# Eleven RMS norms in a two-block model: rows scaled and then transposed, instead of products with a diagonal of 1/rms

## The chip, the cores and the metric

The kernel runs on one core of a Trainium2 chip. The metric is the device time of one execution in microseconds. Before the change three executions took 2910.46, 2912.77 and 2920.75 us; their median, 2912.77 us, is the time to beat. A difference of 0.5% is 14.6 us.

The engines are named as in the profile. PE is TensorE's matrix multiply and PEld its weight load, DVE is VectorE, ACT is ScalarE, POOL is GpSimd, and SP issues most loads.

## The reference, cut to what matters

The model has two blocks of two layers each, on 256 tokens of width 1024, all in float32. Each layer has a mixer and a feed-forward part, and each of these starts with the same step:

```python
def rms_norm(x, g):
    y = x * lax.rsqrt(jnp.mean(x * x, axis=-1, keepdims=True) + EPS)
    return y * g
h = rms_norm(x, norm_g) * (1.0 + scale) + shift      # scale, shift: per channel
proj = h @ w                                         # or the two products of SwiGLU, or the router
```

The sum of squares runs over the channels of one token, so 1/rms is one number per token. The gain, scale and shift are one number per channel. The matrix product that follows sums over channels, so `h` is wanted with channels on the 128 partitions, while `x` is kept with tokens on the partitions.

First block: layer 0 has a dense SwiGLU, layer 1 a mixture of eight experts. The second block has an attention-like mixer with a decaying state; it runs once over a second input (the context) and then over the first block's output (the latent stream).

## The kernel before, in words

`x` lies in four tiles `xs[t][n]`, token half `t` (128 tokens) by channel half `n` (512 channels); in the trace all of them are `xpt`. A norm has these steps, and there are eleven of them in the program:

- `rstd_rows` (L285): for each `t`, two squares with a running sum on ACT (L269, 128x512), then a Newton iteration on DVE for 1/rms (L275 to L281), one number per partition, `r[t]`.
- `scaled_t` (L334): DVE makes two diagonal 128x128 matrices, identity times `r[t]` (L338, tile `g0t` or `g1t`). For each of four groups `kp` of 256 channels PE makes four products, channel block by token half, of a block of `xs` with the diagonal (L344). That turns the block and scales it in one step, into one PSUM bank, 128 channels x 2 x 256 tokens.
- `affine_f32` (L311): A * ps + B per channel; DVE takes the first block of the group (L317) and ACT the second (L320). Both write one tile, and in the trace ACT follows DVE.
- `split` (L295): the result is divided in a rounded high part (ACT, L296) and a remainder (DVE, L297). Every large product is then three products (L234, L239, L240). The weights go through the same two lines as they arrive.

The order of work on every engine is set by a scheduler when the kernel is built: it takes the streams of instructions with their priorities and simulates time to decide what is issued next. The first block and the latent stream have the priority `lead`; the context stream and the vectors of modulation (L388, L410) are `fill`, put where the lead stream would wait. A change in one step can therefore move work in other places.

Tiles come from pools with fixed numbers of buffers. `scaled_t` takes its diagonal from the pool `g` (3 buffers). The tiles of `affine_f32` and `sumsq` come from the stream's pool `st`, and the high and low parts from `s`. In the first block and in the feed-forward part of the latent stream's first layer both are the pool `s0` with 12 buffers; the PSUM tiles come from pools of two banks or one.

Three other places matter below. L1512 to L1545 are the decaying attention of the context (PE L1512, exponentials on ACT at L1515, products L1535 and L1543, then L1575 and its square on ACT, L1577). L660 and L661 are the last step of the first block's mixer, with SiLU on ACT. L824 is the branch behind the router of the experts; behind it the first expert gathers its tokens (L909, L917) and loads its weights (L211).

Of the kernel before, what the change touches and what calls it, by code (L numbers as in the profile page):

```python
# [13 lines left out]
AF = mybir.ActivationFunctionType  # L14
# [48 lines left out]
class Res:  # L63
    """buffers of one stream: pools to take each kind of tile from (the listed ones in turn)"""
# [14 lines left out]
class Task:  # L79
    """a generator of instructions with its buffers and its place in the order of issue"""  # L80
# [15 lines left out]
class Builder:  # L96
# [36 lines left out]
    def use(self, res, key):  # L133
        """what is issued next belongs to the stream key, which takes its buffers from res"""
        if self.key is not None:
            self.prio[self.key] = self.tc.cur_priority
        self.R, self.key = res, key
        self.tc.cur_priority = self.prio[key]

# [77 lines left out]
    def wparts(self, dram):  # L217
        """loads dram [128, kt, n]; yields (first k, its k count, high part, low part), 4 KiB a part"""
        kt, n = dram.shape[1], dram.shape[2]
        st = max(1, 1024 // n)  # L220
        for k0 in range(0, kt, st):
            ks = min(st, kt - k0)
            src = self.wload(dram[:, k0:k0 + ks])
            h, l = (self.shaped(self.htile(), (ks, n)) for _ in range(2))
            self.split(h, l, src)
            yield k0, ks, h, l

    def mm3(self, ps, lh, ll, rh, rl, first, last, start=None):
        """ps += (lh + ll)^T (rh + rl) but for ll^T rl. start: whether the first product clears the marks of its bank;
        a second group in a bank starts without, after the first one's start"""  # L230
        mm = self.nc.tensor.matmul
        before = self.mark
        skip = start is not None
        i = mm(ps, lh, rh, start=start if skip else first, stop=False, skip_group_check=skip)  # L234
        if first:
            self.mark = i
            if start is False:
                self.tc.add_manual_dep(i.ins, before.ins.name, LATE, reason="order of the starts in a bank")
        mm(ps, lh, rl, start=False, stop=False, skip_group_check=skip)  # L239
        mm(ps, ll, rh, start=False, stop=last, skip_group_check=skip)  # L240

    def late(self, dma):
        """holds a load back until the product issued last has begun"""
        self.tc.add_manual_dep(dma.ins, self.mark.ins.name, LATE, reason="buffers of loads that could go far ahead")

# [1 line left out]
    def half_rsqrt(self, h, w):  # L247
        """1 / sqrt(2 h): three Newton steps, each of which turns the sign, from a negative guess"""
        V = self.nc.vector
        j = self.m1(w, I32)  # L250
        V.tensor_scalar(j, h.bitcast(I32), -0.5, float(0x5F3759DF - 0x400000 - 2 ** 31), op0=ALU.mult, op1=ALU.add)
        y = j.bitcast(F32)
        for _ in range(3):
            t, z = self.m1(w), self.m1(w)
            V.tensor_tensor(t, y, y, op=ALU.mult)
            V.tensor_tensor(t, t, h, op=ALU.mult)
            V.scalar_tensor_tensor(z, t, 1.5, y, op0=ALU.subtract, op1=ALU.mult)
            y = z
        return y
# [6 lines left out]
    def sumsq(self, x, out):  # L266
        """half the mean square of 512 of the 1024 columns"""
        j = self.st(512)
        self.nc.scalar.activation(j, x, AF.Square, scale=math.sqrt(0.5 / D), accum_out=out)  # L269

    def rstd(self, ss):
        """1/rms of tokens from the two halves of sumsq, [128, 2]: half_rsqrt with a number for each partition"""
# [12 lines left out]
    def rstd_rows(self, xs):  # L285
        """xs[t][n] [128,512] token-major; 1/rms per token, [128, 1] for each t"""
# [24 lines left out]
    def affine_f32(self, ps, kp, Aff, Bff, pool=None):  # L311
        """ps [128, 2, w] -> A*ps+B"""
# [21 lines left out]
    def scaled_t(self, xs, r):  # L334
        """channel-major xs * r, two blocks of channels at a time: products with diagonals of r"""
        dg = self.shaped(self.g1(), (2, 128))
        for t in range(2):
            self.nc.vector.tensor_scalar(dg[:, t], self.cc("ident"), r[t], None, op0=ALU.mult)  # L338
        for kp in range(4):
            ps = self.tp(2, 256)  # L340
            for q in range(2):
                k = 2 * kp + q
                for t in range(2):
                    self.nc.tensor.matmul(ps[:, q, t * 128:(t + 1) * 128],  # L344
                                          xs[t][k // 4][:, (k % 4) * 128:(k % 4 + 1) * 128], dg[:, t],
                                          start=True, stop=True)
            yield ps
# [6 lines left out]
    def conds(self):  # L354
        """silu of the three conditions, [128, 8, 32]: second block's two, first block's, zeros"""
# [16 lines left out]
    def gemv_step(self, m, c, A, name, l, grow):  # L372
        """a twelfth of the 6144 columns, in four column groups of the tensor engine"""
# [6 lines left out]
    def shift_scale(self, m, b, q, w_dram):  # L380
        """128 columns of each half of shift and scale: a column group each, then to channels on partitions"""
# [17 lines left out]
    def gate_row(self, m, b, half, w_dram, b_dram, grow):  # L399
        """half a gate, to a row in DRAM; each column group takes two of the eight k blocks.  # L400
        grow: function giving a DRAM row to multiply it by, or None"""
# [25 lines left out]
    def affine(self, m, which, i, gname):  # L427
        """(A, B) of g * (1 + scale), shift; which 0: mixer, 1: ffn"""
# [13 lines left out]
    def proj_parts(self, H, w, n, evac, kind="a"):  # L442
        """token-major [2 x 128, n] = H^T-stationary product with w [128, 8, n], in parts"""
# [19 lines left out]
    def ffn(self, H, gu, dn, nu, part, size=2):  # L463
        """SwiGLU over 256 tokens; part(section, t, n, psum) gets the product of each section of the hidden units"""
# [5 lines left out]
        def unit(u):  # L470
            """hidden units on partitions: gate and up blocks of 128, two of each to a bank"""
# [40 lines left out]
    def wout(self, M, w, korder, done, both=False):  # L512
        """mixed^T (M, 8 k blocks) @ w; done(n, [ps0, ps1]). both: the first k blocks for both halves of the columns
        before the others"""
# [29 lines left out]
    def mixer1(self, l, H, M):  # L544
# [10 lines left out]
        # convolution branch, channels on partitions  # L555
# [30 lines left out]
        # gating branch  # L586
# [26 lines left out]
        # gating products  # L613
# [25 lines left out]
        # convolution, layer norm over channels, swish  # L639
# [29 lines left out]
    def conv(self, l, glu):  # L669
        """depthwise convolution of the rows of glu. A product takes 32 channels at eight-apart taps on the rows of  # L670
        the tensor engine, by diagonals of the filters, to a column group of it"""
# [159 lines left out]
    def overflow(self, xn, Aff, Bff, pos, cw, G, xs):  # L831
        """slots 128..255 of each expert, in the buffers of the weights alone"""
# [49 lines left out]
    def scatter(self, pn, ws, G, y, yh, yl, DT, xs, n):  # L882
        """x += the rows of an expert, weighted and gated, back at their tokens"""
# [9 lines left out]
    def experts(self, xn, Aff, Bff, pos, cw, G, xs):  # L893
        """SwiGLU of each expert over the tokens whose slot lies in 0..127; x += their weighted and gated sum"""
# [4 lines left out]
        def gather(e):  # L899
            """tokens of an expert: one-hot rows the other way, their weights, the split inputs"""  # L900
# [134 lines left out]
    def plan(self, xs, m, m2, sh, task, G0, G1, G2, G3):  # L1035
        R0, R1, RM, RL = self.R0, self.R1, self.RM, self.RL

        def weave(t, *others, label="end"):
            """runs t to its label, with steps of the others between its own"""
# [3 lines left out]
        # second stream: modulation, then the whole first layer of the context  # L1043
# [15 lines left out]
        # first block  # L1059
# [30 lines left out]
    def first_end(self, xs):  # L1090
        """final norm of the first block"""
# [37 lines left out]
    def add_norm_gated(self, xs, yg, ss):  # L1129
        """x += rms_norm(y) * gate, from y * gate and the squares of y"""  # L1130
# [54 lines left out]
    def transpose4(self, src, n, w=128):  # L1185
        """src [128 tok, n * w] -> psum [w, n, 128]"""
# [5 lines left out]
    def lower_bounds(self):  # L1192
        """lower bounds of the forget gates of layer 1, one row per direction"""
# [19 lines left out]
    def mixer2(self, l, H, sh, M, kind):  # L1213
# [19 lines left out]
        def rot(o, ps, t):  # L1233
            """rotary embedding of 256 columns"""
# [88 lines left out]
        def take_logs():  # L1323
            """of the forget gates; with a lower bound of zero: log sigmoid(z) = min(z, 0) + log(1 - sigmoid(-|z|))"""
# [10 lines left out]
        def keys():  # L1335
            """keys with features on partitions: 4 (head, map) of 32 per group; the context's go to DRAM"""
# [111 lines left out]
    def state(self, d, lf, kt, v, sh):  # L1448
        """final state of one direction, [128 key, 4 heads, 128 value], to DRAM"""
# [142 lines left out]
    def mixed(self, M, k0, ps, now):  # L1592
        """two k blocks of the mixed branches, split now or by wout"""
# [8 lines left out]
    def transposed(self, ys, p0):  # L1602
        """columns p0 * 128.. of token-major ys[t] -> psum [128, 2, 256]"""
# [94 lines left out]
def _kchunks(w, n):  # L1698
    """[1024, C*n] -> [C, 128, 8, n]"""
# [4 lines left out]
def _level_patterns():  # L1704
    """[128, 2 directions, 9 * 128]: column t of a pattern sums the log decays between t and its block's middle.
    levels 64..8, outer for tokens 0..127, levels 4..1, outer for tokens 128..255"""
# [171 lines left out]
```

## Time and profile before

| | |
|---|---|
| three executions | 2910.46, 2912.77, 2920.75 us |
| span of the profiled execution, first to last instruction | 2917.1 us |
| mean granted clock of TensorE | 0.977 |
| PE busy | 2771.0 us, 95% |
| DVE busy | 2025.3 us, 69% |
| ACT busy | 1700.4 us, 58% |
| DMA, mean over the span | 244 GB/s |

The profile shows the execution from its first instruction to its last; it gives no time outside that span, and the span lies inside the range of the three timed executions, 0.15% above their median. A granted clock of 1.00 is the higher level, 2.4 GHz, and 0.5 the lower, 1.2 GHz. A float32 product of 128x128 is two records in the trace; a transpose is one.

### The profile page before, as it was taken

To read this page: it belongs to the slowest core of one execution; us is meant where nothing else is said; L and a number is where in the kernel's file an instruction comes from. 1 tells how busy PE (TensorE), PEld (TensorE's weight loads), DVE (VectorE), ACT (ScalarE), POOL (GpSimd) and SP (SyncE) were. 2 spreads that over 40 slices of the span, in tenths; PEclk is the share of its full clock that TensorE was granted. 3 is DMA by queue.
4 is the path that set the end of the run, shared out by engine and by line. 5 is a ranking of instruction groups with operands and counts; after the bars stand their busy time and mean duration, and the time that the engine had idled before them with its cause. 6 is when DMAs were issued, how large, how long until landed. Compare 5 with 4: busy or idle time off the path is not lost.

```text
span 2917.1 us, 46050 instructions
## 1 busy us (share of the span) xinstructions
PE 2771.0 (95%) x17334; PEld 2295.3 (79%) x17334; DVE 2025.3 (69%) x3099; ACT 1700.4 (58%) x2353; POOL 77.8 (3%) x144
## 2 busy tenths in 40 slices
PE   6999999998899999999999999998999999799898
PEld 5767788776788888887878888876667989677897
DVE  3535555656777878789899998985566555666555
ACT  3435445545566666666777777775445554654543
POOL 0110000010000000000000000000000000000000
PEclk8999999999999999999999999999989999899999
DMA  9987766642688888888999999996563556324463
GB/s 358 338 298 234 250 198 225 222 127 84 224 307 296 295 282 299 298 290 313 350 354 339 350 347 360 355 361 210 167 211 110 182 171 189 118 66 132 152 185 112
DMA packets 202954, 711.71 MB, mean 244 GB/s; under 512 B 24506, under 2 KB 28730, under 8 KB 202720
## 3 DMA queue, kind: packets, MB, share of 16 engines
q1 hardware_dynamic: 196112, 692.82, 69.6%
q0 software_dynamic: 6320, 15.30, 1.8%
q8 instruction: 138, 2.26, 0.3%
q14 instruction: 96, 0.79, 0.1%
q10 hardware_dynamic: 288, 0.55, 0.1%
HBM read 704.49 MB, written 4.08 MB: 243 GB/s over the span
## 4 chain that ended last, share of the span: by engine, by line
PE 65%; DVE 3%; ACT 2%; DMA 2%; issue 1%; DVEq 0%; SPq 0%; ACTq 0%; POOLq 0%
PE a0t L234 8%; PE a0t L239 8%; PE a0t L240 8%; PE a1t L239 6%; PE a1t L240 6%; PE a1t L234 6%; PE t0t L239 5%; PE t0t L240 5%; PE t0t L234 5%; PE a1t L1512 1%; PE t0t L1535 1%; ACT h0t L296 1%; DVE h0t L297 1%; PE t0t L344 1%; PE t2t L909 1%
## 5 line engine op out<-in xcount | busy, mean ns | idle before, releaser
L296 ACT CAST h0t<-w0t 128x1024 fp32r<-128x1024 f32 (+1 forms) x505 | 525.4, 1043 | 386.1 <-PE a0t L239 243.8
L297 DVE TENSOR_TENSOR h0t<-w0t,h0t 128x1024 fp32r<-128x1024 f32 (+1 forms) x302 | 364.9, 1209 | 264.7 <-ACT h0t L296 247.5
L234 PE MATMUL a0t<-s0t,h0t 128*128 128x256 f32 x800 | 225.9, 287 | 4.4 <-ACT h0t L296 2.1
L239 PE MATMUL a0t<-s0t,h0t 128*128 128x256 f32 x800 | 224.2, 284 | 0.0
L240 PE MATMUL a0t<-s0t,h0t 128*128 128x256 f32 x800 | 220.1, 286 | 0.5 <-DVE h0t L297 0.5
L296 ACT CAST h1t<-w1t 128x1024 fp32r<-128x1024 f32 x155 | 162.9, 1051 | 96.1 <-PE a1t L239 44.6
L239 PE MATMUL a0t<-h0t,s2t 128*128 128x512 f32 x492 | 193.8, 396 | 0.0
L240 PE MATMUL a0t<-h0t,s2t 128*128 128x512 f32 x466 | 181.0, 394 | 0.0
L297 DVE TENSOR_TENSOR h2t<-w0t,h0t 128x1024 fp32r<-128x1024 f32 x122 | 149.1, 1222 | 29.9 <-ACT h0t L296 22.3
L234 PE MATMUL a0t<-h0t,s2t 128*128 128x512 f32 x466 | 167.4, 399 | 1.0 <-DVE s0t L1176 0.5
L234 PEld LDWEIGHTS a0t<-s0t,h0t 128*128 128x128 f32 x800 | 153.0, 192 | 13.1 <-issue 4.5
L296 ACT CAST h0t<-w1t 128x1024 fp32r<-128x1024 f32 x120 | 126.2, 1052 | 49.4 <-PE a1t L240 17.4
L239 PEld LDWEIGHTS a0t<-s0t,h0t 128*128 128x128 f32 x800 | 153.6, 192 | 1.6 <-issue 0.8
L240 PEld LDWEIGHTS a0t<-s0t,h0t 128*128 128x128 f32 x800 | 150.0, 192 | 4.2 <-DVE h0t L297 1.9
L234 PE MATMUL t0t<-h0t,s0t 128*128 128x512 f32 x374 | 147.1, 393 | 1.9 <-ACT h0t L296 1.9
L239 PE MATMUL t0t<-h0t,s0t 128*128 128x512 f32 x372 | 147.7, 397 | 1.3 <-DVE h0t L297 1.3
L240 PE MATMUL t0t<-h0t,s0t 128*128 128x512 f32 x374 | 147.5, 394 | 0.0
L297 DVE TENSOR_TENSOR h1t<-w0t,h0t 128x1024 fp32r<-128x1024 f32 x81 | 98.9, 1221 | 25.1 <-ACT k0t L483 6.6
L297 DVE TENSOR_TENSOR h1t<-w1t,h1t 128x1024 fp32r<-128x1024 f32 x80 | 97.7, 1222 | 23.9 <-ACT h1t L296 21.8
L239 PE MATMUL a1t<-s1t,h1t 128*128 128x256 f32 x408 | 113.7, 283 | 0.0
L234 PE MATMUL a1t<-s1t,h1t 128*128 128x256 f32 x408 | 113.4, 283 | 0.0
L297 DVE TENSOR_TENSOR h0t<-w0t,h1t 128x1024 fp32r<-128x1024 f32 x80 | 97.7, 1221 | 20.0 <-ACT k0t L483 5.0
(740 smaller groups left out, 7453.2 us busy)
## 6 DMA issues: line engine op xcount, KB each, us to landing
w0t<-in_mgu_dram SPq DMA_DIRECT2D x306, 512.0 KB, 5.5
w0t<-in_mdn_dram SPq DMA_DIRECT2D x152, 512.0 KB, 5.2
w1t<-in_mgu_dram SPq DMA_DIRECT2D x107, 512.0 KB, 5.7
w0t<-in_f2gu_dram SPq DMA_DIRECT2D x66, 512.0 KB, 3.9
w1t<-in_f2gu_dram SPq DMA_DIRECT2D x61, 512.0 KB, 4.8
w1t<-in_win_dram SPq DMA_DIRECT2D x54, 512.0 KB, 4.9
w1t<-in_mdn_dram SPq DMA_DIRECT2D x54, 512.0 KB, 5.4
w1t<-in_mod_s_dram SPq DMA_DIRECT2D x48, 512.0 KB, 6.2
```

Of the source, the lines that this page charges most:

```text
L234: i = mm(ps, lh, rh, start=start if skip else first, stop=False, skip_group_check=skip)
L239: mm(ps, lh, rl, start=False, stop=False, skip_group_check=skip)
L240: mm(ps, ll, rh, start=False, stop=last, skip_group_check=skip)
L296: self.nc.scalar.copy(out_h, src)
L297: self.nc.vector.tensor_sub(out_l, src, out_h)
L344: self.nc.tensor.matmul(ps[:, q, t * 128:(t + 1) * 128], xs[t][k // 4][:, (k % 4) * 128:(k % 4 + 1) * 128], dg[:, t], start=True, stop=True)
L909: nc.tensor.matmul(ps[:, q], xn[t][k0 // 4][:, q * 128:q * 128 + 128], Dt[:, t], start=t == 0, stop=t == 1)
L1512: nc.tensor.matmul(pe[:, h].rearrange("p a b -> p (a b)"), x[:, (h0 + h) * 128:(h0 + h + 1) * 128], rhs, start=i == 0, stop=i == 1)
L1535: nc.tensor.matmul(ps[:, h], L[:, h], R[:, h], start=True, stop=True)
```

## The change

`scaled_t` no longer makes diagonals. For each channel half it scales the rows, half of the tokens on DVE and half on ACT, into two new tiles of 512 channels from the pool `st`. Then it turns each 128x128 block with a transpose, a product with the constant identity in a mode that only moves values. The rest of the norm is as before. In the changed file all comments are gone as well, which leaves lines empty, and lines behind `scaled_t` have numbers greater by four.

```diff
     def scaled_t(self, xs, r):
-        dg = self.shaped(self.g1(), (2, 128))
-        for t in range(2):
-            self.nc.vector.tensor_scalar(dg[:, t], self.cc("ident"), r[t], None, op0=ALU.mult)
-        for kp in range(4):
-            ps = self.tp(2, 256)
-            for q in range(2):
-                k = 2 * kp + q
-                for t in range(2):
-                    self.nc.tensor.matmul(ps[:, q, t * 128:(t + 1) * 128],
-                                          xs[t][k // 4][:, (k % 4) * 128:(k % 4 + 1) * 128], dg[:, t],
-                                          start=True, stop=True)
-            yield ps
+        for n in range(2):
+            xn = []
+            for t in range(2):
+                y = self.st(512)
+                if t == 0:
+                    self.nc.vector.tensor_scalar(y, xs[t][n], r[t], None, op0=ALU.mult)
+                else:
+                    self.nc.scalar.activation(y, xs[t][n], AF.Copy, scale=r[t])
+                xn.append(y)
+            for kp in range(2):
+                ps = self.tp(2, 256)
+                for q in range(2):
+                    c = (2 * kp + q) * 128
+                    for t in range(2):
+                        self.nc.tensor.transpose(ps[:, q, t * 128:(t + 1) * 128], xn[t][:, c:c + 128], self.cc("ident"))
+                yield ps
```

In the changed file L341 is the scaling on DVE, L343 that on ACT and L350 the transpose.

The first place is ACT in the norm before the last feed-forward part (2712 us of the trace): L320 is the affine step, L296 the high part. Before:

```order
L320 ACTIVATE s0t_36440<-t0t_36435,bff_36402,aff_36400 128x256
L296 CAST s1t_36443<-s0t_36440 128x512
L320 ACTIVATE s0t_36452<-t0t_36447,bff_36402,aff_36400 128x256
L296 CAST s1t_36455<-s0t_36452 128x512
L320 ACTIVATE s0t_36464<-t0t_36459,bff_36402,aff_36400 128x256
```

Now:

```order
L343 ACTIVATE s0t_36484<-xpt_136,m0t_36473 128x512
L320 ACTIVATE s0t_36491<-t0t_36486,bff_36452,aff_36450 128x256
L343 ACTIVATE s0t_36512<-xpt_138,m0t_36473 128x512
L296 CAST s1t_36494<-s0t_36491 128x512
L320 ACTIVATE s0t_36503<-t0t_36498,bff_36452,aff_36450 128x256
L296 CAST s1t_36506<-s0t_36503 128x512
```

The scaling of the second channel half stands between the first group's affine step and its high part.

The second place is ACT at the end of the first block's second mixer (660 us), with the context's attention in `fill`. L661 (now L665) is the lead's SiLU, L1515 (L1519) the context's exponential. Before:

```order
L661 ACT_TABLE_LOAD
L661 ACTIVATE s0t_7392<-t0t_7391,ppt 128x256
L1515 ACT_TABLE_LOAD
L1515 ACTIVATE w1t_2844<-a1t_2845 128x2x2x128
L1515 ACTIVATE w1t_2844<-a1t_2851 128x2x2x128
L661 ACT_TABLE_LOAD
L661 ACTIVATE s0t_7392<-t0t_7391,ppt 128x256
L296 CAST s0t_7399<-s0t_7392 128x512
L1515 ACT_TABLE_LOAD
L1515 ACTIVATE w2t_2857<-a1t_2858 128x2x2x128
L661 ACT_TABLE_LOAD
L661 ACTIVATE s0t_7404<-t0t_7403,ppt 128x256
```

Now:

```order
L1519 ACTIVATE w1t_2875<-a1t_2882 128x2x2x128
L296 CAST h2t_3027<-w1t_3025 128x1024
L1549 COPY s1t_2933<-t1t_2928 128x512
L296 CAST h1t_3045<-w1t_3043 128x1024
L1549 COPY s1t_2940<-t2t_2935 128x512
L1581 ACTIVATE s3t_2952<-a1t_2943 128x512
L1581 ACTIVATE s3t_2964<-a1t_2955 128x512
L665 ACT_TABLE_LOAD
L665 ACTIVATE s0t_7412<-t0t_7411,ppt 128x256 x2
```

All exponentials and the context's last squares (L1577, now L1581) now stand ahead of the SiLU; six table loads have become one here.

The third place is PE right behind the branch (750 us): t0t is the lead's first expert, a1t the context's feed-forward part. Before:

```order
L824 UNCONDITIONAL_BRANCH x2
L909 MATMUL t2t_19741<-s3t_19720,s0t_7657 128x128
L909 MATMUL t2t_19741<-s3t_19720,s0t_7661 128x128
L909 MATMUL t2t_19741<-s3t_19720,s0t_7657 128x128
L909 MATMUL t2t_19741<-s3t_19720,s0t_7661 128x128
```

Now:

```order
L828 UNCONDITIONAL_BRANCH x2
L234 MATMUL a1t_17841<-s1t_17808,h1t_17875 128x256
L239 MATMUL a1t_17841<-s1t_17809,h1t_17875 128x256
L234 MATMUL a1t_17842<-s1t_17808,h1t_17875 128x256
L239 MATMUL a1t_17842<-s1t_17809,h1t_17875 128x256
L350 MATMUL t1t_17828<-cct,s1t_17812 128x128
```

The context's norm, which stood behind the branch, now stands mostly ahead of it, and 24 of its feed-forward products stand between the branch and the gather's second half (L909, now L913); another 24 stand ahead of the branch.

## Rows read from the trace of the kernel before

**Rows 1.** The page's first part: busy time, share of the span and instructions.
```profile
PE 2771.0 (95%) x17334; PEld 2295.3 (79%) x17334; DVE 2025.3 (69%) x3099; ACT 1700.4 (58%) x2353; POOL 77.8 (3%) x144
```

**Rows 2.** Stretches: length, busy PE, PEld, DVE, ACT, POOL; clock, DMA share, GB/s.
```profile
0.00:100.00 100.00, 75.92 (x946) 58.01 (x946) 38.15 (x100) 37.85 (x70) 8.09 (x24) 0.86 0.96 361
100.00:660.00 560.00, 545.53 (x4369) 433.38 (x4368) 310.04 (x602) 266.98 (x400) 41.37 (x67) 1.00 0.69 228
660.00:682.00 22.00, 13.00 (x75) 11.49 (x76) 14.41 (x41) 16.66 (x23) 0.00 (x0) 0.77 0.15 48
740.00:764.00 24.00, 14.72 (x66) 12.83 (x67) 14.49 (x58) 10.05 (x22) 0.00 (x0) 0.84 0.48 162
2490.00:2506.00 16.00, 7.24 (x37) 6.78 (x37) 12.16 (x46) 6.77 (x16) 0.54 (x1) 0.57 0.22 75
```

**Rows 3.** Stretches of L344 on PE alone: first, a filled norm, an exposed norm.
```profile
30.00:46.00 16.00, 6.36 (x32) 0.70 1.01 395
716.00:730.00 14.00, 4.39 (x32) 1.00 0.40 116
2498.00:2507.00 9.00, 6.68 (x32) 0.67 0.03 6
```

**Rows 4.** Timeline of PE: start, length; a group's products, four transposes, context products.
```profile
724.68 1.05 PE L344 MATMUL t2t<-g0t,xpt 128*128 128x128 f32 x8
...
433.18 0.60 PE L1189 MATMUL t1t<-cct,s3t 128*128 128x128 f32 x4
...
780.64 0.28 PE L239 MATMUL a1t<-s1t,h1t 128*128 128x256 f32 x1
780.75 0.28 PE L240 MATMUL a1t<-s1t,h1t 128*128 128x256 f32 x1
```

**Rows 5.** Instructions by line: shortest, median, longest in ns; first and last start.
```profile
L338 DVE TENSOR_SCALAR g0t<-cct,m0t x16: 277/282/288, 30.0 to 2713.0; 128x128 f32<-128x128 f32 x16
...
L305 DVE TENSOR_SCALAR s0t<-xpt,m0t x2: 478/479/480, 729.9 to 730.3; 128x512 f32<-128x512 f32 x2
...
L307 ACT ACTIVATE s0t<-xpt,m0t x2: 712/713/714, 729.4 to 730.0; 128x512 f32<-128x512 f32 x2
```

**Rows 6.** Timeline of the last norm, idle time before in brackets.
```profile
2712.57 3.48 PE L344 MATMUL t0t<-g0t,xpt 128*128 128x128 f32 x16 [8.66 <-DVE m0t L281]
...
2712.98 0.29 DVE L338 TENSOR_SCALAR g0t<-cct,m0t 128x128 f32<-128x128 f32 x1
2715.09 0.54 DVE L317 TENSOR_SCALAR s0t<-t0t,aff,bff 128x256 f32<-128x256 f32 x1 [1.82 <-PE t0t L344]
2715.73 0.56 ACT L320 ACTIVATE s0t<-t0t,bff,aff 128x256 f32<-128x256 f32 x1 [4.60 <-DVE s0t L317]
...
2716.32 0.62 ACT L296 CAST s1t<-s0t 128x512 fp32r<-128x512 f32 x1
...
2716.98 0.69 DVE L297 TENSOR_TENSOR s1t<-s0t,s1t 128x512 fp32r<-128x512 f32 x1 [0.34 <-ACT s1t L296]
2717.26 0.36 PE L234 MATMUL a0t<-s1t,h0t 128*128 128x256 f32 x1
```

**Rows 7.** Timeline of ACT and PE at the end of the second mixer.
```profile
663.72 1.16 PE L1535 MATMUL t2t<-s3t,s3t 128*128 128x128 f32 x8 [1.72 <-DVE s3t L1532]
...
670.53 1.28 ACT L1515 ACT_TABLE_LOAD   x1
...
672.48 1.22 PE L1512 MATMUL a1t<-levt,s3t 128*128 128x256 f32 x4 [3.70 <-ACT w2t L1515]
```

**Rows 8.** Timeline of ACT and PE at the branch.
```profile
753.52 1.28 ACT L269 ACT_TABLE_LOAD   x1 [6.19 <-ACTq L824]
...
756.89 3.41 PE L909 MATMUL t2t<-s3t,s0t 128*128 128x128 f32 x16 [3.66 <-ACT s2t L917]
...
762.25 0.50 PE L234 MATMUL t0t<-h0t,s0t 128*128 128x512 f32 x1 [1.94 <-ACT h0t L296]
```

## The prediction

> **What bounds the kernel now.** I read the busy times first: PE is busy for 2771 of 2917 us, ACT for 58%, DVE for 69% [rows 1]. Then the stretches, because the eleven norms lie in stages with different limits [rows 2]. In the first 100 us the DMA engines are 96% busy and PE only 76%: there the loads set the time. From 100 to 660 us PE is busy for 545.5 of 560 us at a clock of 1.00: there each microsecond of PE work is a microsecond of time. Around 2490 us it is neither: PE is busy for 7.2 of 16 us at a clock of 0.57, waiting for the chain of a norm.
>
> So I sort the norms by PE's idle time around their products. Two lie in the first 100 us (at 35 and 90 us). Six are filled, that is, other products stand between theirs: at 240, 540, 716, 768, 2217 and 2250 us. Three are exposed, with nothing else for PE: at 1980, 2499 and 2713 us.
>
> **PE's own work.** A group's eight records of L344 take 1.05 us at the full clock; four transposes of the same size elsewhere in this kernel take 0.60 us [rows 4], so a group saves 0.45 us and a norm of four groups 1.8 us. The filled norm at 716 us agrees, with 4.39 us for its 32 records [rows 3]. The Trainium skill (TensorE: Matmul & The Clock Gate, Terms) calls the transpose mode four times faster for float32. By that a group would save 0.79 us and the six filled norms 19 us; the rows show a ratio of 1.75, tail included, and the measurement decides.
>
> - Six filled norms: 24 groups x 0.45 = 10.8 us saved, on the path.
> - Two norms at the start: 8 groups x 0.45 = 3.6 us of PE work, beside saturated loads. I take 0, and the range keeps 0 to 3.6.
>
> **The exposed norms.** I follow the last one [rows 6]. Before: the second diagonal starts at 2712.98, DVE begins the first affine step at 2715.09, and the first product with the result starts at 2717.26. Now 1/rms of the second half comes up to 0.20 us later, since a scaling of 0.48 us stands in DVE's queue in place of a diagonal of 0.28 [rows 5]: 2713.18. ACT's scaling takes 0.71 [rows 5], to 2713.89. Four transposes at the half clock take about half of what the eight records took, which I estimate at 1.0 us from the 6.68 us that 32 records took at a clock of 0.67 [rows 3]: 2714.9, or 0.2 us earlier than before. But on ACT the second channel half's scaling now stands between the affine step and the high part (first piece of the order), so from 2714.9: 0.54 + 0.1 + 0.56 + 0.71 + 0.62 = 2717.4, that is, 0.2 us later. The fourth group then takes 0.45 us less of PE, so the norm gains 0.2 us. At 2499 and 1980 us PE itself was the last to be ready (its first three groups ran at the half clock), and I put 0.6 us on each. Together 1.4 us, with bounds of -1.5 (in each the 0.71 us of a scaling uncovered, less the 0.2) and +6 (in each half of the 6.68 us saved, less one scaling and one high part).
>
> **What ACT and DVE get.** ACT gains 22 scalings of 0.71 = 15.7 us, DVE 22 x (0.48 - 0.28) = 4.4 us [rows 5]. In the filled norms both engines have idle time, and other products cover them. The weak point is the second channel half: from its scaling to its first product it needs 0.71 + 0.60 + 0.54 + 0.56 + 0.62 = 3.0 us, and it takes two more buffers from a pool of 12. In the order of the changed kernel, 10 to 13 lead or context products stand between its transposes and its first use in the filled norms, 1 to 3 us. I take -1 us in all; the bound is six times 3.0 less 1 us of cover, -12.
>
> **What the order moves.** Two other places change.
>
> - At 660 us ACT alternated between SiLU and exponential, a table load of 1.28 us each time, while PE waited up to 3.70 us for an exponential [rows 7]. PE was idle for 9.0 of 22 us there, at a clock of 0.77 [rows 2]. Now the exponentials come first and two loads do (second piece). The whole 9.0 us could go. Against that, the tail of the context's attention now stands ahead of the lead's output products, where before these ran between its pieces. Each of its groups shows a wait of about 1.7 us when nothing is between [rows 7], and there are about four: -6.8. I take +3, with both ends kept: -6.8 to +9.
> - At the branch PE was idle for 9.3 of 24 us [rows 2], 3.66 and 1.94 us of it right behind [rows 8]. Now 48 context products of 0.12 us, by the distance of their starts [rows 4], stand on both sides of it: 5.8 us of work moved into idle time. ACT also no longer has two squares of the context ahead of the gather's affine step. Against it stands one more table load of 1.28 us ahead of the router's exponential. I take +3, bounds -1.3 to +5.8.
>
> **The sum.** 10.8 + 0 + 1.4 - 1 + 3 + 3 = 17.2 us. Against the profiled execution: 2917.1 - 17.2 = 2899.9 us of span. That execution is 4.3 us above the median of the timed ones, and the trace tells no time outside the span, so I take the sum off the median: 2912.8 - 17.2 = 2895.6 us, 0.6% faster.
>
> **Rivals.**
>
> 1. The clock stays low through the exposed norms. Before, PE's clock was back soon after the products began: 0.67 over 2498 to 2507 us [rows 3]. If only the real products behind the transposes bring it back, it returns about 4 us later in each of the three, and PE's work in these 4 us takes 2 us more: 6 us, hence 2901.6. For it: no row shows transposes alone behind an idle PE. Against it: the transposes of rows 4 stand in a stretch at 1.00. The Trainium skill (TensorE: Matmul & The Clock Gate, Part 4) says that the higher level does not engage for transposes; by that rule it is this rival that happens, and no row here decides it.
> 2. The order gives nothing and the second half takes some: the two moved places come out at 0, and the filled norms lose 5 us to the late second half. 10.8 + 1.4 - 5 = 7 us: 2905.6. For it: both moved places are trades of one wait for another. This is also where it ends if the filled norms are less bound by PE than their stretches say.
> 3. Slower: the second channel half comes uncovered in all nine norms past the start. Then each pays its 3.0 us, and PE, idle so long, drops to the half clock, as it does around the 3.66 us wait at the branch, where the 16 records take 3.41 us [rows 8] against 2.1 for two groups of eight [rows 4], 1.3 us more. 9 x 4.3 = 38.7 us against 17.2 saved: 21.5 us slower, 2934. It beats the saving as soon as more than 1.9 us per norm is uncovered; the products I see behind the transposes speak against it in most norms, the shared pool of 12 buffers for it.
>
> **How the numbers follow.** Forecast 0.52, rival 1 0.12, rival 2 0.22, rival 3 0.14. 0.5% (14.6 us) is about what a measurement of this kernel can tell from no change. The faster edge is at 2898.2, only 2.6 us above the forecast, and its own range is 2880 to 2911 (both moved places at an end). Faster: 0.52 x 0.72 + 0.12 x 0.3 + 0.22 x 0.15 = 0.44. Slower: 0.14 x 0.85 + a little of rival 2, 0.13. Same: the rest, 0.43. The range leaves out most of rival 3: 2877 to 2922.
>
> **What would show it.** L350 has 176 records of about 4.4 x 0.60 / 1.05 = 2.5 us per norm at the full clock. The idle time in 660 to 682 us falls from 9.0 to about 5, that at the branch from 9.3 to about 6. In the last norm the first product with the result starts 4.5 to 5 us after the first 1/rms. I am wrong if PE shows new waits of over 1.5 us for L296, L297 or L341 in the filled norms (rival 3 or 2), if the clock in 2490 to 2506 us is clearly below 0.57 (rival 1), or if PE's idle time moves by 10 us or more at a place that I don't name, since the order changed in many places of the first 1340 us.

## The result: 0.5% slower

The changed kernel takes 2927.8 us, median of four executions (2927.1 to 2934.1); the kernel before took 2911.6 (2909.7 to 2920.8). The ratio is 1.0052, 95% interval 1.0035 to 1.0070. The forecast was 2895.6 us, its range 2877 to 2922: wrong by 32 us, and on the wrong side.

In the changed kernel L344 is L350, and lines behind it have numbers greater by four. Page of the profile after, part 1, beside [rows 1]:

```profile
span 2926.4 us, 45733 instructions
...
PE 2765.7 (95%) x17158; PEld 2276.4 (78%) x17158; DVE 2025.8 (69%) x3099; ACT 1708.6 (58%) x2372; POOL 77.1 (3%) x144
```

PE works 5.3 us less and the span is 9.3 us longer. The profiled execution of before was a long one: a second trace of the old form (first experiment) spans 2909.5 us. From here on the changed kernel is compared with that trace: 16.9 us longer.

L350 alone in four of the eleven norms (beside [rows 3]); columns: stretch, its length, PE busy and records, PEld, granted clock, DMA share, GB/s:

```profile
239.00:256.00 17.00, 3.21 (x16) 2.43 (x16) 0.79 0.62 193
545.00:562.00 17.00, 2.14 (x16) 1.70 (x15) 1.00 0.62 201
...
2507.00:2516.00 9.00, 4.37 (x16) 3.02 (x16) 0.51 0.01 3
2715.00:2730.00 15.00, 4.34 (x16) 2.94 (x16) 0.66 0.09 33
```

At the full clock a norm takes 2.14 us, where the products took 4.39 [rows 3]. So PE's own saving is there. I divided PE's time without overlap (each record counts from the end of the one before it) and subtracted the second trace of the old form. "To the experts' end" is the last record of the experts, at 1966.1 us in the old form, 1985.6 in the changed one. Times in us:

| kernel | stage | waits | the norms' records | all other records | sum |
|---|---|---|---|---|---|
| changed | to the experts' end | +9.2 | -7.5 | +17.8 | +19.5 |
| changed | behind it | +6.6 | -10.1 | +0.4 | -3.1 |
| before, its own trace | to the experts' end | +1.0 | +3.1 | -0.3 | +3.7 |
| before, its own trace | behind it | +0.8 | -0.1 | +3.2 | +3.9 |

The last two rows are the same program twice: some 4 us in each stage are only the difference between executions. The norms' records save 17.6 us; the first 1986 us give back 27, more than the whole. Busy time times (1 - granted clock), over stretches of 4 us, is 14.8 us larger there, so the half clock can account for most of the +17.8. That it does is not shown: in the first trace of before this measure is 10.5 us larger too (9 us of it in the first 100 us), and the other records take no longer there. Where the time goes, in the old form (first fence) and the changed kernel (second); columns: stretch, length, busy us and count of PE, PEld, DVE, ACT, POOL, granted clock, DMA share, GB/s:

```profile
200.00:300.00 100.00, 97.10 (x812) 76.19 (x813) 61.35 (x134) 54.20 (x96) 6.61 (x13) 1.00 0.77 257
...
540.00:600.00 60.00, 60.00 (x423) 49.10 (x422) 27.11 (x35) 32.98 (x47) 3.15 (x6) 1.00 0.53 165
600.00:820.00 220.00, 193.99 (x1226) 164.06 (x1225) 155.78 (x365) 118.45 (x179) 13.33 (x16) 0.95 0.51 161
820.00:1380.00 560.00, 553.22 (x2952) 472.73 (x2951) 456.12 (x515) 374.11 (x460) 1.07 (x2) 1.00 0.88 298
```

```profile
200.00:300.00 100.00, 93.17 (x733) 70.92 (x732) 52.34 (x125) 49.15 (x90) 5.35 (x10) 0.91 0.67 220
...
540.00:600.00 60.00, 56.82 (x396) 46.49 (x395) 31.27 (x57) 35.63 (x53) 5.02 (x9) 1.00 0.50 167
600.00:820.00 220.00, 196.08 (x1235) 165.61 (x1234) 148.63 (x354) 111.05 (x173) 12.29 (x16) 0.93 0.47 152
820.00:1380.00 560.00, 546.71 (x2878) 461.16 (x2877) 446.71 (x509) 367.51 (x454) 1.07 (x2) 1.00 0.85 291
```

**Place one, 200 to 300 us**, around the norm of the dense feed-forward: 3.9 us more waits, and a clock of 0.91. PE first waits 2.9 us for a load of the context's gates (at 234 us), and the clock falls to 0.50 until about 246 us (first fence). Then it waits again. Timeline of DVE, ACT and PE there (second fence: start, duration, instruction; idle time before and what ended it in brackets):

```profile
242.00:246.00 4.00, 4.00 (x16) 1.90 (x17) 1.94 (x6) 2.33 (x5) 0.00 (x0) 0.50 0.56 176
246.00:250.00 4.00, 4.00 (x30) 2.60 (x29) 1.68 (x4) 2.09 (x4) 0.53 (x1) 0.99 0.50 153
```

```profile
234.32 2.26 PE L414 MATMUL a1t<-w1t,conds 128*32 128x256 f32 x16 [2.88 <-DMA w1t<-in_mod_g_dram]
...
259.75 0.62 ACT L296 CAST s0t<-s0t 128x512 fp32r<-128x512 f32 x1
...
264.03 0.68 DVE L423 TENSOR_TENSOR k1t<-t1t,k1t 2x512 f32<-2x512 f32 x1 [4.58 <-DMA k1t<-in_mod_b_dram]
...
265.10 0.68 DVE L297 TENSOR_TENSOR s0t<-s0t,s0t 128x512 fp32r<-128x512 f32 x1
...
265.84 0.38 PE L239 MATMUL a0t<-s0t,h0t 128*128 128x256 f32 x1 [3.06 <-DVE s0t L297]
```

The high part of the norm's last group is ready at 260.4 us. Its remainder (L297) is a task of 0.7 us, but DVE holds an addition for a gate of the context (L423) ahead of it, and that waits 4.6 us for a load. In this second wait no step of the norm is slow; an instruction of another stream stands in its queue.

**Place two, 540 to 1380 us**: 3.2 us more waits around the norm of the second layer's mixer, 2.1 us less from 600 to 820 at a lower clock (0.93 for 0.95), and 6.5 us more from 820 to 1380, in the experts, where no norm stands.

### The profile page after: what moved, and what is told of

It is laid out like the page before. It is cut to its first block, busy times and chain, and to the rows that moved or that the text cites. A ratio compares the mean times of both kernels' runs of the same rounds, so it can differ in the third digit from the quotient of the medians.

```text
span 2926.4 us, 45733 instructions
## 1 busy us (share of the span) xinstructions
PE 2765.7 (95%) x17158; PEld 2276.4 (78%) x17158; DVE 2025.8 (69%) x3099; ACT 1708.6 (58%) x2372; POOL 77.1 (3%) x144
## 4 chain that ended last, share of the span: by engine, by line
PE 62%; DVE 4%; DMA 4%; ACT 3%; issue 1%; SPq 0%; DVEq 0%; ACTq 0%; POOLq 0%
PE a0t L234 8%; PE a0t L239 8%; PE a0t L240 8%; PE a1t L239 6%; PE a1t L240 6%; PE a1t L234 6%; PE t0t L239 4%; PE t0t L240 4%; PE t0t L234 4%; DMA w0t<-in_mdn_dram 1%; DVE h0t L297 1%; ACT h0t L296 1%; PE a1t L1516 1%; PE t0t L1539 1%; DMA w1t<-in_mod_s_dram 1%
## 5 line engine op out<-in xcount | busy, mean ns | idle before, releaser
L296 ACT CAST h0t<-w0t 128x1024 fp32r<-128x1024 f32 (+1 forms) x505 | 525.9, 1043 | 388.0 <-PE a0t L239 242.6
L297 DVE TENSOR_TENSOR h0t<-w0t,h0t 128x1024 fp32r<-128x1024 f32 (+1 forms) x302 | 364.9, 1208 | 277.7 <-ACT h0t L296 246.7
L296 ACT CAST h1t<-w1t 128x1024 fp32r<-128x1024 f32 x155 | 162.9, 1051 | 108.1 <-PE a1t L239 54.8
L297 DVE TENSOR_TENSOR h2t<-w0t,h0t 128x1024 fp32r<-128x1024 f32 x122 | 148.8, 1220 | 28.9 <-ACT h0t L296 20.7
L296 ACT CAST h0t<-w1t 128x1024 fp32r<-128x1024 f32 x120 | 126.2, 1052 | 48.8 <-PE a1t L240 17.5
L297 DVE TENSOR_TENSOR h0t<-w0t,w2t 128x1024 fp32r<-128x1024 f32 x81 | 98.9, 1221 | 33.7 <-ACT w2t L296 33.1
L297 DVE TENSOR_TENSOR h1t<-w0t,h0t 128x1024 fp32r<-128x1024 f32 x81 | 98.8, 1220 | 26.4 <-ACT h0t L296 6.6
L297 DVE TENSOR_TENSOR h1t<-w1t,h1t 128x1024 fp32r<-128x1024 f32 x80 | 97.6, 1220 | 22.9 <-ACT h1t L296 21.0
```

The costliest lines, as they stand in the source:

```text
L296: self.nc.scalar.copy(out_h, src)
L297: self.nc.vector.tensor_sub(out_l, src, out_h)
```

## Experiments

Two theories stood against each other. **Order theory**: the steps of the new form save time, and what costs is the new order that the scheduler makes of all streams around them. **Norm theory**: each norm past the start pays for its late second channel half (rival 3 in a milder size).

For the experiments both forms stand in one file, and a list of names says where the new one is used: `c0m`, `c0f` (context), `b0m`, `b0f`, `b1m`, `moe` (first block's two mixers, its feed-forward, the experts), `l0m`, `ck`, `l0f`, `l1m`, `l1f` (from 1980 us on). The scheduler orders each kernel anew. A kernel's name below is its label.

```diff
+LB_LAYER = 1; NEW = ('b1m',)
-    def scaled_t(self, xs, r):
+    def scaled_t(self, xs, r, site):
+        if site not in NEW: yield from diag_t(self, xs, r); return
```

**e0_all_old**, `NEW = ()`.

> All eleven norms in the old form (products with a diagonal), written in the file in which single norms can be switched; the order of instructions is that of the kernel before. Every theory: the time of before, 2909 to 2914 us. Its profile is a second look at the old form: the one profiled execution of before may not be a typical one. If so, the stretches in which this trace is shorter than that of before by more than 2 us are no effect of the change.

2911.7 us, ratio 1.0007 (0.9991 to 1.0023); before, beside it, 2905.6 to 2920.5. As expected, and its trace is the better one to compare with.

**e1_only_b1m**, `NEW = ('b1m',)`.

> New form in one norm alone, that of the mixer of the first block's second layer (at 540 us); the other ten old. On PE the order then differs from before only between this norm and a little past the branch to the experts. Order theory (the shift of 14 to 17 us at the branch comes from the order behind this one norm: the context's attention stands ahead of the lead's mixer, and the experts behind it are bound by their loads, so the delay stays): 2923 to 2930 us, 12 to 18 us slower than before. Norm theory (each norm past the start pays for its late second channel half, 1.5 to 2 us net): 2911 to 2915 us.

2923.7 us, ratio 1.0037 (1.0024 to 1.0049): one norm of eleven costs 10 us, at the near end of what the order theory said (2923 to 2930). It holds here against the norm theory.

**e2_all_but_b1m**, the other ten.

> New form in ten norms, old in the mixer of the first block's second layer. Order theory: nearly the whole loss goes, 2905 to 2913 us; the first load of an expert starts within 4 us of 757 us, where it stood before. Norm theory: nine tenths of the loss stay, 2923 to 2928 us.

2920.2 us, ratio 1.0029 (1.0018 to 1.0040). Between the two theories: `b1m` is not all of it. The first expert load comes at 762.9 us, 10 later than in the old form (753.1) and outside the 4 us that were expected, and the delay arises between 185 us (1.7 late by a landmark of the context on PE) and 342 us (12.8 late): place one.

**e3_late_five**, `NEW = ('l0m', 'ck', 'l0f', 'l1m', 'l1f')`.

> New form in the five norms of the second block past the experts (at 1980, 2217, 2250, 2499 and 2713 us), old in the six before; the order of the first 1970 us is that of before. Order theory: the five save about 10 us of PE work and give back up to 6 in waits, so 2904 to 2911 us. Norm theory: five of the nine norms that pay, 2917 to 2922 us. If the clock stays low through the three exposed norms: 6 us of it, 2913 to 2918 us, and a granted clock clearly under that of the old form around these norms.

2908.7 us, ratio 0.9986 (0.9975 to 0.9996): 5 us faster. The norm theory is wrong here too. By the division above, behind the experts: waits +6.0, the norms' records -10.6, all other -4.3.

Now the decisive pair for place two. **e4_b1m_by_half** is e1 with the four scalings dealt out otherwise:

```diff
-                if t == 0:
+                if n == 1:
```

> New form in the norm of the mixer of the first block's second layer alone, as in the run of that norm before, but the four scalings are dealt out the other way: ACT takes both token halves of the first channel half, DVE both of the second. Same instructions, same count on each engine. The scheduler then leaves the context's attention behind the lead's mixer and the branch where it stood in the old form (the order differs by 52 rows at the norm and by some 190 ahead of the branch). Order theory: the 10 us of the first run of this norm are gone, 2910 to 2917 us, first load of an expert within 4 us of that of the old form (753 us). Norm theory (the cost is in the steps of the new form): as in the first run, 2920 to 2927 us.

2913.1 us, ratio 0.9991 (0.9982 to 1.0001). The same kinds and numbers of instructions on the same engines, with the scalings dealt out otherwise and another order of everything behind them, and the 10 us are gone. The dealing itself is not what costs: around the norm both wait alike (first lines of the fences below: PE busy for 58.02 and 58.42 of 60 us). The first expert load is issued at 764.4 us in e1, 751.7 in e4 and 753.1 in the old form. In e1, 22 products of the context's feed-forward and 12 of its norm start ahead of the branch that start behind it in the old form, in e4 none, and the context's last load is issued at 1254.9 us; in the old form at 1292.8. That would leave the experts less to fill their waits with. PE of e1 (first fence) and e4 (second); from 820 to 1380 us the old form has 553.22:

```profile
540.00:600.00 60.00, 58.02 (x408) 47.59 (x407) 27.63 (x37) 34.87 (x50) 3.18 (x6) 1.00 0.49 158
820.00:1380.00 560.00, 545.93 (x2874) 460.63 (x2874) 447.08 (x510) 368.01 (x453) 1.07 (x2) 1.00 0.86 291
```

```profile
540.00:600.00 60.00, 58.42 (x407) 47.85 (x406) 27.24 (x34) 32.40 (x47) 3.16 (x6) 1.00 0.52 168
820.00:1380.00 560.00, 549.38 (x2916) 466.80 (x2915) 452.42 (x513) 372.10 (x457) 1.08 (x2) 1.00 0.87 295
```

e4 keeps the branch in its place but lies between (last load of the context at 1268.6 us), so the lost filling is one part of the 10 us, not shown to be all. e4 also has the first of the two moved places of the prediction, at 660 us: ACT makes all exponentials of the context ahead of the SiLU there, with one table load. What e1 has and e4 has not is above all the second, the branch; ahead of it, from some 560 us on, the two orders differ as well.

**e5_eight**, all but `b0m`, `b0f`, `b1m`.

> New form in eight norms: all but the three of the first block's mixers and of its dense feed-forward. The order of the first 760 us is that of the old form but for the norms themselves. Order theory: the five late ones gave -5 us; the norm of the experts (filled, about 1.5 us of PE) and the two of the context add -3 to 0: 2904 to 2910 us. Norm theory: the norm of the experts and the second one of the context pay 1.5 to 2 us each, 2911 to 2915 us.

2909.9 us, ratio 0.9988 (0.9977 to 0.9998). Within the order theory's span, but no further than with five: the three early norms added nothing that can be measured.

Place one: which of the two norms makes it? **e6_old_b0m_b1m** has nine new, **e7_old_b0f_b1m** too.

> New form in nine norms; old in the mixers of both layers of the first block. With ten new norms (only the second layer's mixer old) the lead stream lost 11 us between 185 and 342 us: PE waited 2.6 us for a load of a gate at 233 us and went on at the half clock for some 16 us, and 2.8 us at 267 us for a low part that stood in DVE's queue behind an addition waiting for a load. Theory A: this comes from the order that the first layer's mixer norm makes (the lead runs 9 us ahead by 188 us, and so the gates' loads are late at the next norm): then it goes here, clock near 1.00 from 230 to 260 us, 2903 to 2911 us. Theory B: it comes from the new form of the feed-forward's norm itself, whose transposes do not bring the clock back: it stays, 2914 to 2921 us.

> New form in nine norms; old in the first block's dense feed-forward and in the mixer of its second layer, new in that of its first. Theory A (the order that the first layer's mixer norm makes): the loss between 185 and 342 us stays, 2913 to 2921 us. Theory B (the new form of the feed-forward's norm): it goes, since products with a diagonal stand there again, and the clock is near 1.00 from 230 to 260 us; 2903 to 2911 us.

2912.3 us, ratio 0.9990 (0.9979 to 1.0002), and 2910.1 us, 0.9989 (0.9979 to 0.9999). Both are rid of it (e6 ends 1 us above its range), so neither A nor B is right alone. With e5 and e2, which have both of these norms old and both new, the four cases are complete: 0.9988, 0.9990, 0.9989 and, with both new, 1.0029. PE of e7 stands in the order of e2 up to the norm (240 us), waits for the same loads, and still recovers. PE there in e7 (products with a diagonal, first fence) and e2 (transposes, second):

```profile
234.00:238.00 4.00, 3.15 (x25) 0.96 (x25) 0.60 (x3) 0.00 (x0) 0.00 (x0) 0.60 1.02 381
238.00:242.00 4.00, 4.00 (x28) 2.57 (x21) 0.44 (x3) 1.27 (x5) 0.00 (x0) 0.55 0.85 310
242.00:246.00 4.00, 4.00 (x30) 2.55 (x30) 2.40 (x6) 2.40 (x6) 0.55 (x1) 1.00 0.50 149
```

```profile
238.00:242.00 4.00, 3.96 (x21) 1.91 (x17) 0.49 (x2) 0.92 (x4) 0.00 (x0) 0.50 0.93 323
242.00:246.00 4.00, 4.00 (x19) 2.28 (x19) 0.77 (x2) 2.00 (x5) 0.00 (x0) 0.50 0.68 211
246.00:250.00 4.00, 4.00 (x15) 1.07 (x13) 2.12 (x6) 1.18 (x2) 0.53 (x1) 0.50 0.18 68
250.00:254.00 4.00, 4.00 (x24) 2.96 (x24) 1.68 (x3) 2.08 (x4) 0.00 (x0) 0.56 0.59 173
```

With products the clock is back at about 241.6 us, 7.7 us behind the end of the first wait (233.9); with transposes at about 253.5, 18 us behind it (235.5). And e7 has no second wait. In e6, with the old form in `b0m`, the clock stays at 1.00 from 230 to 260 us. So it takes both: in the order that the new `b0m` makes, PE waits 2 us and more at a time for the gates' loads (1.5 at most in e6), and with the new `b0f` behind that the time is not made good.

**e8_clock_alone** takes the clock by itself, behind the end of the program:

```diff
+    turn(160); wait(); product(80); wait()
+    turn(40); product(40); wait(); product(40); turn(40)
```

> Old form in all norms, and behind the last product of the program five stretches on PE alone, each behind some 8 us in which PE waits for a chain on DVE: 160 transposes; 80 float32 products of 128x128; 40 transposes and then 40 products; 40 products and then 40 transposes (the first wait stands behind 4 transposes). What they make is not used. Clock theory (transposes do not bring the clock back after an idle wait, products do): the 160 transposes run at 0.50 to their end, 0.2 us each, some 34 us; the 80 products get back to 1.00 within about 8 us; in the third stretch the clock returns only behind the transposes. Rival (the clock comes back with PE's work of either kind): both stretches return within the same 4 to 8 us. The whole time is some 130 us more and says nothing.

One execution. PE's timeline (L1911 transposes, L1915 products; a product is two records), and below it three stretches with the clock:

```profile
2916.51 20.25 PE L1911 MATMUL t0t<-cct,s0t 128*128 128x128 f32 x160 [8.83 <-DVE s0t L1907]
2944.93 20.12 PE L1915 MATMUL t0t<-cct,s0t 128*128 128x128 f32 x160 [8.17 <-DVE s0t L1907]
2973.21 6.13 PE L1911 MATMUL t0t<-cct,s0t 128*128 128x128 f32 x40 [8.16 <-DVE s0t L1907]
```

```profile
2920.00:2924.00 4.00, 4.00 (x30) 4.00 (x29) 0.00 (x0) 0.00 (x0) 0.00 (x0) 0.77 0.02 4
2948.00:2952.00 4.00, 4.00 (x33) 4.00 (x32) 0.00 (x0) 0.00 (x0) 0.00 (x0) 0.86 0.00 0
2976.00:2980.00 4.00, 4.00 (x37) 4.00 (x36) 0.00 (x0) 0.00 (x0) 0.00 (x0) 0.95 0.00 0
```

160 records of either kind take about the same (20.25 and 20.12 us). The granted clock is 0.50 at first in each; by these stretches it reaches 1.00 some 5.3 us behind the first of the 160 transposes, 4.2 us behind the first product, and in the third stretch 3.2 us behind the first of 40 transposes, with nothing but transposes so far. The clock theory as I wrote it falls: a dense run of transposes does bring the clock back. What kept it down for 17 us in e2 is a mix of transposes, products of 32 columns and gaps; what in the mix does it was not tried.

**e9_more_pe_in_experts** asks why time lost early stays lost:

```diff
-                for q in range(2):
-                    nc.tensor.transpose(pt[:, q], a[:, q * 128:q * 128 + 128], idn)
+                for q in range(6 if e > 3 else 2):
+                    nc.tensor.transpose(pt[:, q % 2], a[:, q % 2 * 128:q % 2 * 128 + 128], idn)
```

> Old form in all norms; in the last four of the eight experts each of the 14 units of hidden channels makes its two transposes three times over (the same result): 224 transposes more in the stretch from about 1360 to 1960 us, where the old form shows PE busy for 630 of 645 us and the DMA engines at 0.96. At 0.11 us each that is 24 us of PE work. Load theory (the experts last as long as their loads, so PE time saved or lost there is nothing, and a late start is kept to the end): 0 to 6 us slower than before. PE theory (PE is the bound there, as its busy share says): 15 to 24 us slower.

2934.1 us, ratio 1.0060 (1.0046 to 1.0075): 17.5 us slower by the ratio, for 24 us of work. My load theory falls. The experts' loads keep the DMA engines 97% busy in the old form and 95% here, but PE is the bound there too, as its busy share says (576 of 580 us in both). This fits that a delay of the first 750 us arrives at the end.

**e10_ten**: new in all but `b0f`; `b0m` and `b1m` dealt out by channel half as in e4.

> New form in ten norms, old in the first block's dense feed-forward; in the two mixers of the first block the scalings are dealt out by channel half (ACT the first, DVE the second) instead of by token half. Both orders that cost time are avoided. Order theory: 2905 to 2911 us, as with nine. Norm theory: ten of eleven norms pay, 2920 to 2928 us.

2909.5 us, ratio 0.9986 (0.9976 to 0.9995): with e3 the fastest, 5 us under before.

**e11_all_by_half_b**: all eleven new, the three of the first block by channel half.

```diff
-                if t == 0:
+                if (n == 1 if site[0] == 'b' else t == 0):
```

> New form in all eleven norms, as in the changed kernel, but in the three norms of the first block the scalings are dealt out by channel half. Same instructions on each engine as in the changed kernel. The order behind the second layer's mixer norm is the good one (branch where it stood in the old form); ahead of the feed-forward's norm the order is that of the changed kernel, so the wait for the gates' loads at 232 us and the half clock behind it should stay, without the addition ahead of the last low part in DVE's queue. Order theory: 2909 to 2917 us, at least 10 us faster than the changed kernel. Norm theory: 2924 to 2930 us, like the changed kernel.

2914.4 us, ratio 0.9996 (0.9986 to 1.0006). The changed kernel's engines do the same work, and the time is 13 us under its 2927.8 (16 by the ratios), by another dealing of the scalings in three norms and the order that follows from it. At place one the wait for the gates' loads (3.6 us) and the half clock stay, as expected; the wait behind L423 does not (0.3 us in its place).

Where the 13 us lie is told by three landmarks that all kernels share: PE's first record of L1629 (at 184.8 us in e0), that of L1460 (446.0), and the last record of the experts (1966.1). Place one lies between the first two, place two between the last two. How much later than in e0 each comes, in us:

| kernel | L1629 | L1460 | experts' end |
|---|---|---|---|
| changed | -0.4 | +8.9 | +19.5 |
| e2 (`b1m` old) | +1.7 | +12.9 | +10.3 |
| e7 (`b0f`, `b1m` old) | +1.7 | +2.0 | +3.3 |
| e1 (only `b1m`) | -0.5 | +2.1 | +15.0 |
| e4 (only `b1m`, by half) | +0.4 | +2.2 | +5.6 |
| e11 (all, by half) | +6.7 | +11.0 | +8.5 |
| before, its own trace | -0.8 | +3.5 | +3.7 |

So the changed kernel loses 9 us at place one and 11 at place two. e11 loses 7 us ahead of both and 4 at place one, and nothing at place two; that is where it gains on the changed kernel. What costs it the 7 us was not looked for. As the last row shows, some 4 us can be chance.

## Why the prediction was wrong

- **PE's own work** was right in size. Forecast: 10.8 us in six filled norms, up to 3.6 at the start, and at the upper bound half of PE's time in the exposed ones. Measured: 17.6 us less in the norms' records, 2.14 us per norm at the full clock for the 2.5 forecast. As time it shows only behind the experts: e3 is 5 us faster, and e5, e6 and e7, with three and four early norms more in the new form, are no faster than e3 (ratios 0.9988, 0.9990 and 0.9989 for 0.9986). So 10.8 us "on the path" was PE's work and not time, even in the good orders.
- **The exposed norms**: forecast -1.4 us, found about +0.4 in the last one: from PE's first record to the end of the first 18 records of products with the result it takes 8.41 us, in the old form 7.97. In the norm at 2499 us this loss is 0.4 us too (11.09 for 10.73). Timeline of the last one in the changed kernel, beside [rows 6]:

```profile
2720.22 0.48 DVE L341 TENSOR_SCALAR s0t<-xpt,m0t 128x512 f32<-128x512 f32 x1
...
2720.85 0.66 PE L350 MATMUL t0t<-cct,s0t 128*128 128x128 f32 x2 [8.84 <-DVE m0t L281]
...
2722.09 1.54 PE L350 MATMUL t0t<-cct,s0t 128*128 128x128 f32 x6 [0.58 <-ACT s0t L343]
...
2724.13 0.47 DVE L341 TENSOR_SCALAR s0t<-xpt,m0t 128x512 f32<-128x512 f32 x1
...
2724.75 1.09 PE L350 MATMUL t0t<-cct,s0t 128*128 128x128 f32 x4 [1.12 <-DVE s0t L341]
...
2725.49 0.56 PE L234 MATMUL a0t<-s1t,h0t 128*128 128x256 f32 x1
```

  From PE's first record to the first product with the result it takes 4.64 us, before 4.69 [rows 6]. From the first scaling, which starts as the first 1/rms is ready, it takes 5.27 us; forecast were 4.5 to 5. PE's saving turned into waits here (0.58 and 1.12 us in the lines above), and behind the experts as a whole the waits are 6.6 us longer where the norms' records are 10.1 us shorter. The first product takes 0.56 us for 0.36: PE is still at the half clock. The clock in the last norm, the changed kernel and e0:

```profile
2727.00:2729.00 2.00, 2.00 (x17) 2.00 (x17) 1.41 (x4) 1.89 (x4) 0.00 (x0) 0.87 0.00 0
```

```profile
2707.00:2709.00 2.00, 1.76 (x10) 1.57 (x10) 1.03 (x2) 0.87 (x2) 0.00 (x0) 0.72 0.00 0
```

  It is back near 2727.5 us, 6.7 us behind the first transpose; in e0 near 2708.1, 3.2 us behind its first product with the diagonal. Rival 1 is right that the clock comes back later, here by 3.5 us for its 4, and the two norms that were looked at end with a small loss instead of a gain. At 1980 us the norm was not exposed as the prediction read it: products of the modulation (L388) stand between its own, and PE waits 4.4 us there for a load of theirs; the half clock around it lasts 13.7 us in e0 and in the changed kernel alike. The Trainium skill (TensorE: Matmul & The Clock Gate, Part 4) says that the higher level does not engage for transposes; e8 shows it engage, at 1.00 for the last 15 of 20 us of nothing else.
- **The order** is the step that failed: +3 and +3 for two moved places, with bounds of -6.8 and -1.3, and nothing for the rest. I looked at the order where the diff of the two orders touched something I had already read in the profile, and took the rest as equal. At both places the waits did fall. At the table alternation PE is busy for 11.30 of 22 us in the old form and 14.10 in the changed kernel (5 us of wait were forecast, 7.9 are left). At the branch it goes from 9.2 us of idle time in 24 to 4.2, where 6 were forecast (e0 in the first fence, the changed kernel in the second, both from 10 us ahead of the branch):

```profile
737.00:761.00 24.00, 14.79 (x67) 12.78 (x66) 14.56 (x56) 10.62 (x21) 0.00 (x0) 0.82 0.48 164
```

```profile
757.00:781.00 24.00, 19.81 (x119) 18.46 (x118) 13.28 (x36) 14.51 (x21) 0.00 (x0) 0.76 0.37 137
```

  These waits were not time saved: the order that brings the branch's filling costs 10 us (e1 against e4), where the sum has +3, in part because the work that filled it is missing later (3.5 us more waits in e1 than in e4 from 820 to 1380 us). The other part is the norm at 240 us, which the sum carries as a plain saving: it lost 3.9 us of waits and 7 us of clock.
- **Rival 3**, the slower one, has the right sign and comes nearest in time (2934), but with the wrong mechanism, so that its nearness is luck. It charges nine norms for a late second channel half. One filled norm shows such a wait, the one at 240 us, and there the cause is L423 in DVE's queue; e11 has the same second halves without that wait, and 13 us less.
- **Rival 2** is what the good orders come to: e3, e5, e7 and e10 are 3 to 5 us faster than before, and its 2905.6 was 7 us under.
- The text did name what would prove it wrong, a wait of over 1.5 us for L297 in a filled norm, and 10 us of idle time at a place not named. The first came (3.06 us), though behind L423. PE's idle time rose by 3.9 us at place one and by 6.5 in the experts, each under those 10, while each place cost some 10 us in all. Rival 1's sign, a clock clearly below 0.57 in the norm at 2499 us, came weakly: 0.53 over 16 us, 0.58 in e0.
- **Open**: how the 10 us of place two divide. From L1460 to the experts' end e1 takes 9.5 us more than e4; of it some 4.5 us are waits (3.5 of them from 820 to 1380 us), the rest longer records, in part at the half clock. Single traces differ by 4 us in such a stage.

## What to carry to other kernels

Where a scheduler orders all engines, a local saving of some 2 us per place is smaller than what a new order does (here 13 us between two orders of the same work). So first price the order: build two or three forms that are equal in work and see whether they move the same other streams, and measure them all. And read a filled stretch for what fills it: work of another stream put earlier can be missing later.

## What the runs showed of the hardware that was not expected

- After an idle wait of 8 us, 160 transposes took 20.25 us and 160 records of float32 products 20.12, with the half clock first and the full clock from 5.3 and 4.2 us on (e8, one execution).
- In a mix with small products the clock was back some 8 us behind the wait with products with a diagonal (e7, e10) and 12 to 18 us behind it with transposes (changed kernel, e11, e2); what in the mix made the difference was not tried.
- With the DMA engines at 97% and PE at 99% of 580 us, 24 us of added PE work cost 17.5 us (e9), and the DMA share fell to 95%: there a share near the full one did not mean that the loads set the time.
